# Another program order for the second layer of a two-layer hybrid decoder: score chunks, transposes and products placed by time

## The chip, the cores and the metric

The kernel runs on one core of one Trainium2 chip. Five engines work beside each other, each on its own queue of instructions: PE (TensorE: matmuls and transposes, with its weight loads shown apart as PEld), DVE (VectorE), ACT (ScalarE), POOL (GpSimd) and SP, which here issues DMAs. The metric is the device time of one execution in microseconds (us), the median over runs. A profile is of a single execution; its span is counted from its first to its last instruction.

## The reference, cut to what matters

The input is 1024 rows of 1024 numbers. Layer 1 is differential attention with eight heads. After it one K and V are projected, and layer 2 is stick-breaking attention with sixteen heads of 64, which the kernel takes in eight pairs. Both layers multiply by a SiLU gate, project and add the residual.

```python
def block(args):                      # of _stick_breaking
    i, qb = args
    qpos = i * QB + jnp.arange(QB)
    mask = kpos[None, :] < qpos[:, None]
    z = jnp.einsum('bhqd,bshd->bhqs', qb, k).astype(jnp.float32) * scale
    log_beta = jax.nn.log_sigmoid(z)
    log_1mb = jnp.where(mask, jax.nn.log_sigmoid(-z), 0.0)
    suffix = lax.cumsum(log_1mb, axis=3, reverse=True) - log_1mb
    a = jnp.where(mask, jnp.exp(log_beta + suffix), 0.0)
    return jnp.einsum('bhqs,bshe->bhqe', a.astype(v.dtype), v)
```

## The kernel before, in words

Every fp32 operand is split into a high and a low part, and a product is three matmuls (high by high, high by low, low by high). In this text a **head** of layer 2 is one pair of reference heads, c = 0 and c = 1.

**Units.** The 1024 query rows are eight blocks of 128, numbered qb. Unit m (0 to 3) takes the blocks 2m and 2m+1, and block qb has n = (qb+1)·128 columns of scores. A block over 512 columns has its scores in two chunks, later columns first (`chunks`, `scores`, L237), one chunk at a time in the one score tile of PSUM (`sc`, two banks). ACT copies a chunk into `zl` tiles (L781), POOL masks its end (L783). Then comes a chain over the whole block: DVE L790, ACT L791, ACT L792, DVE L793, the scan on DVE L795, and ACT L796, which leaves the weights a in the `zl` tile. A block up to 512 columns takes one `zl` tile for both c, a longer one takes two; there are seven (`bl`). The first instruction on a `zl` tile is a small memset on POOL (L775).

**Transposes and products.** `unit_t_b` (S below stands for a unit's scores and chain, T for this) has a step for each c and each pair t of column blocks: up to four transposes (`transposed`, L265) into one of three PSUM banks (`tr`), the high part on ACT (`th`, L271), the low part on DVE (`tl`, L272), and four matmuls into the one bank `av` (L811, L812). `th` and `tl` share three buffers. With the last pair of a c, ACT L817 and DVE L818 take the result out of `av`. A unit has 2(m+1) such pairs, a head 20. Layer 1 has the same structure with six matmuls to a pair and ten pairs a head.

**Projections.** While head h is worked on, head h+1's k, v, q and gate are projected from the layer's input (`group`, L195 to L197, 512 columns a matmul), two PSUM banks `proj`, in that order, each for both halves of the rows. A step of `group` is four of the eight parts of the inner dimension, twelve matmuls. These steps are called the fill. The tiles of k, v and q exist twice, so k of head h+1 takes the tiles that head h-1's scores read, and v the tiles that its products read. ACT (L243) and DVE (L245) take k out of PSUM.

**The order.** `run_layer` writes a program order: for each head `main` holds S and T of the units, T of a unit behind S of the next one, the last T of a head behind the first S of the next head, and `merge` mixes main and fill in proportion to costs that stand beside the steps. Layer 2's unit order is `ORDERS[2]`, (1, 3, 0, 2). `gate_mul` of head h-1 stands behind the first unit's late T in head h. This program order is not yet the order on the engines. When the program is built, a scheduler walks through it with a model of each instruction's time and gives each engine, of the instructions that are ready by that model, the one that is earliest in the program order (`hp()` moves some ahead, `later()` some back). Tiles are given out and come free in that walk too. On the chip each engine then keeps to the order it was given, and waits on semaphores.

**The end.** The last head has a list of its own (`last_order`, for layer 2 (1, 0, 3, 2)), mixed with the output projection (`OutProj`, L424 adds the residual, L436 a remainder); the output projection's own tail follows.

Of the kernel before, what the change touches and what calls it, by code (L numbers as in the profile page):

```python
# [14 lines left out]
I32 = mybir.dt.int32  # L15
AF = mybir.ActivationFunctionType
# [3 lines left out]
P = 128  # L20
# [15 lines left out]
def build(tc, ins, out):  # L36
# [9 lines left out]
         "al": 6, "bl": 7, "tb": 3, "oa": 0, "la": 0, "lb": 8, "lt": 0, "lead": 1.0, "leada": 0.02, "leadb": 0.02, "leadxa": 0.15, "leadxb": 0.1, "holda": 0, "holdb": 0, "c2": 1, "gca": 0, "gcb": 0, "prea": 2, "preb": 1, "warm": 16, "wp": 2, "hpx": -1, "nx": 1, "nk": 6, "hpo": 0, "ob": 2, "late": 400}  # L46
# [37 lines left out]
    def zat(n):  # L84
        return zt()
# [97 lines left out]
    def group(n, pairs, done):  # L183
# [3 lines left out]
        size = 4 if n > 256 else 8  # L187
# [39 lines left out]
    def scores(q, k, i, evac):  # L227

        n = (i + 1) * P
        rs_ = slice((i % 4) * P, (i % 4) * P + P)  # L230
        for off, w in reversed(chunks(n)):
# [7 lines left out]
            evac(off, w, n, pts)  # L239

# [33 lines left out]

    def v_rows(pt):
# [9 lines left out]
    def merge(main, fill, lead=0.0):  # L285
# [4 lines left out]
        while i < len(main) or j < len(fill):  # L290
# [4 lines left out]
            else:  # L295
                df += fill[j][0]
                fill[j][1]()
                j += 1

# [141 lines left out]
    def run_layer(hds, qkv, unit_s, unit_t, xT, og, op, hfs):  # L441
# [66 lines left out]
        for h in range(n - 1):  # L508
            main = []
# [12 lines left out]
        ss = unit_s(h, ma)  # L522
        main = (late + ss if B["lt"] else ss + late) + [(0.0, lambda: gate_mul(hds[h - 1], h - 1, og)),
# [72 lines left out]
    def unit_s_a(h, m):  # L596
        hd = heads_a[h]

        def s_step(qb):
            if hd.o is None:  # L600
                hd.o = [T("o", [P, HALF], B["o"]) for _ in range(2)]
                hd.at = {}
            n = (qb + 1) * P
            p = [zat(n + P), zat(n + P)]
            mn = [small(2), small(2)]

            def evac(off, w, n, pts):
                k = 0 if off == 0 else 1
                mask = mask_a[:, HALF - w:] if off + w == n else mask_a[:, 0:1].to_broadcast([P, w])
                for c in range(2):  # L610
                    dve.tensor_tensor_reduce(p[c][:, off:off + w], pts[:, c, :w], mask, 1.0, BIG, ALU.add, ALU.min,  # L611
                                             mn[c][:, k:k + 1])

            scores(hd.q[qb // 4], hd.k, qb, evac)
            s = small(2)
            for c in range(2):
                b = mn[c][:, 0:1]
                if n > 512:
                    dve.tensor_tensor(b, b, mn[c][:, 1:2], ALU.min)
                act.activation(p[c][:, :n], p[c][:, :n], AF.Exp, bias=b, scale=-1.0, accum_out=s[:, c:c + 1])  # L620
            r = small(2)
            dve.reciprocal(r, s)
            dve.tensor_tensor(r[:, 1:2], r[:, 1:2], nlam, ALU.mult)
            dve.tensor_scalar(p[0][:, :n], p[0][:, :n], r[:, 0:1], None, ALU.mult)
            dve.scalar_tensor_tensor(p[1][:, :n], p[1][:, :n], r[:, 1:2], p[0][:, :n], ALU.mult, ALU.add)
            hd.at[qb] = p[1]

        return [(4 * (qb + 1) * P * 0.42, lambda qb=qb: s_step(qb)) for qb in (2 * m, 2 * m + 1)]

    def unit_t_a(h, m):  # L630
# [3 lines left out]
        def t_step(t):  # L634
# [3 lines left out]
            for i, (kb, th, tl) in enumerate(transposed(hd.at[2 * m], hd.at[2 * m + 1], t, t == m)):  # L638
# [14 lines left out]
        return [(4 * 55 + 6 * 109 + (430 if t == m else 0), lambda t=t: t_step(t)) for t in range(m + 1)]  # L653
# [109 lines left out]
    def unit_s_b(p, m):  # L763
        hd = heads_b[p]

        def s_step(qb):
            if hd.o is None:
                hd.o = [T("o", [P, HALF], B["o"]) for _ in range(2)]
                hd.at = {}
            n = (qb + 1) * P  # L770
            heads = ((0, 1),) if n <= HALF else ((0,), (1,))
            z = [zbt() for _ in heads]
            w2 = len(heads[0]) * n
            for t in z:
                pool.memset(t[:, w2:w2 + 1], 0.0)  # L775
# [10 lines left out]
            scores(hd.q[qb // 4], hd.k, qb, evac)  # L786
            for t in z:
                zc = t[:, :w2]
                u = u4k()[:, :w2]
                dve.tensor_scalar(u.bitcast(I32), zc.bitcast(I32), -0x80000000, None, ALU.bitwise_or)  # L790
                act.activation(u, u, AF.Exp)  # L791
                act.activation(u, u, AF.Ln, bias=1.0)  # L792
                dve.scalar_tensor_tensor(u, zc, 0.0, u, ALU.min, ALU.subtract)  # L793
                ur = u[:, ::-1]
                dve.tensor_tensor_scan(ur, t[:, 1:w2 + 1][:, ::-1], ur, 0.0, ALU.add, ALU.subtract)  # L795
                act.activation(zc, u, AF.Exp, scale=-1.0)  # L796
            hd.at[qb] = [z[0][:, :n], z[0][:, n:2 * n]] if n <= HALF else [t[:, :n] for t in z]

        return [(4 * (qb + 1) * P * 0.42, lambda qb=qb: s_step(qb)) for qb in (2 * m, 2 * m + 1)]

    def unit_t_b(p, m):
# [3 lines left out]
        def t_step(c, t):  # L805
# [3 lines left out]
            for i, (kb, th, tl) in enumerate(transposed(hd.at[2 * m][c], hd.at[2 * m + 1][c], t, t == m)):  # L809
# [12 lines left out]
        return [(4 * 55 + 4 * 109, lambda c=c, t=t: t_step(c, t)) for c in range(2) for t in range(m + 1)]  # L822
# [59 lines left out]
```

## Time and profile before

| what | value |
|---|---|
| median of three runs | 1461.78 us (1460.41 to 1463.3) |
| the profiled execution | 1463.71 us |
| its span | 1461.8 us |
| mean granted TensorE clock | 0.985 of full |
| layer 1's heads, about | 60 to 690 us |
| layer 2's heads, about | 690 to 1407 us |
| output projection's tail | 1407 to 1461.8 us |

The profiled execution is 1.9 us over the median. [...] Matmuls overlap: a 512-column matmul is listed with 0.39 us, and the next one starts 0.23 us after it. So PE can be busy for the whole of a stretch and still do more or less in it; only PE's idle time, the clock and the distance of starts tell.

### The profile page before, as it was taken

The page shows a single profiled execution, that of the slowest core. Times are in us where ns is not written, and L with a number is a line of the kernel's source. Part 1 is how long each engine was busy: PE and PEld are TensorE (multiplying, and loading weights), DVE is VectorE, ACT ScalarE, POOL GpSimd, SP SyncE. Part 2 cuts the span into 40 slices and gives each one's busy share as a digit, 9 for nine tenths or more (in the row PEclk, how much of TensorE's full clock was granted, in tenths as well). Part 3 has the DMA queues.
Part 4 walks back from the last instruction along what each step waited for, and adds up shares of the span by engine and source line. Part 5 has one row for each costly group of instructions (what it writes and reads, how often), then busy time and mean ns, then how long its engine had stood idle before and what let it go on. Part 6 is the DMA issues. An engine that isn't in the chain of part 4 may idle for free.

```text
span 1461.8 us, 24434 instructions
## 1 busy us (share of the span) xinstructions
PE 1409.5 (96%) x8944; PEld 1188.5 (81%) x8944; DVE 1073.2 (73%) x2219; ACT 927.8 (63%) x1908; POOL 294.9 (20%) x545
## 2 busy tenths in 40 slices
PE   8999999999999999999999999998999999987899
PEld 7888888888888888789877777776778677776699
DVE  7576667677777776775547888878878888888952
ACT  7555556566565655442557777778777877787720
POOL 0111212121212121100011222223233232335100
PEclk9999999999999999999999999999999999998999
DMA  5111111111111115621310011110011010233512
GB/s 203 59 30 44 45 44 44 44 44 44 44 44 44 44 61 185 214 90 58 116 58 29 30 58 29 44 44 30 34 45 38 30 58 30 70 133 111 193 73 80
DMA packets 43111, 99.39 MB, mean 68 GB/s; under 512 B 4848, under 2 KB 6640, under 8 KB 41968
## 3 DMA queue, kind: packets, MB, share of 16 engines
q1 hardware_dynamic: 42992, 97.83, 19.5%
q8 instruction: 71, 1.16, 0.3%
q14 instruction: 48, 0.39, 0.1%
HBM read 74.74 MB, written 23.07 MB: 67 GB/s over the span
## 4 chain that ended last, share of the span: by engine, by line
PE 75%; DVE 12%; ACT 6%; issue 4%; DMA 2%; POOL 1%; SPq 0%; DVEq 0%; POOLq 0%; ACTq 0%
PE proj L195 18%; PE proj L196 17%; PE proj L197 17%; PE sc L237 8%; PE tr L265 5%; DVE u4k L795 4%; DVE u4k L793 2%; DVE tl L272 2%; PE av L811 2%; PE av L812 2%; PE av L642 1%; ACT u4k L791 1%; PE av L640 1%; PE av L641 1%; ACT u4k L792 1%
## 5 line engine op out<-in xcount | busy, mean ns | idle before, releaser
L195 PE MATMUL proj<-ah,w 128*128 128x512 f32 x768 | 309.0, 402 | 5.4 <-DVE kl L245 5.3
L196 PE MATMUL proj<-al,w 128*128 128x512 f32 x768 | 308.5, 402 | 0.0
L197 PE MATMUL proj<-ah,w 128*128 128x512 f32 x768 | 306.4, 399 | 0.0
L195 PE MATMUL proj<-w,ah 128*128 128x256 f32 x992 | 291.2, 294 | 5.2 <-DVE kl L424 2.7
L197 PE MATMUL proj<-w,al 128*128 128x256 f32 x992 | 285.4, 288 | 0.0
L196 PE MATMUL proj<-w,ah 128*128 128x256 f32 x992 | 285.2, 288 | 0.0
L195 PEld LDWEIGHTS proj<-w,ah 128*128 128x128 f32 x992 | 192.3, 194 | 15.6 <-DVE kl L424 4.2
L197 PEld LDWEIGHTS proj<-w,al 128*128 128x128 f32 x992 | 192.3, 194 | 1.9 <-issue 1.6
L196 PEld LDWEIGHTS proj<-w,ah 128*128 128x128 f32 x992 | 192.3, 194 | 1.9 <-issue 1.3
L195 PEld LDWEIGHTS proj<-ah,w 128*128 128x128 f32 x768 | 145.6, 190 | 41.4 <-DVE kl L245 6.6
L795 DVE TENSOR_TENSOR_SCAN u4k<-zl,u4k 128x768 f32<-128x768 f32 (+4 forms) x96 | 173.7, 1812 | 1.0
L196 PEld LDWEIGHTS proj<-al,w 128*128 128x128 f32 x768 | 145.7, 190 | 33.0 <-issue 6.4
L197 PEld LDWEIGHTS proj<-ah,w 128*128 128x128 f32 x768 | 145.7, 190 | 32.1 <-issue 4.2
L237 PE MATMUL sc<-kh,q 64*128 64x512 f32 (+2 forms) x768 | 158.2, 400 | 12.6 <-ACT zl L781 9.8
L272 DVE TENSOR_TENSOR tl<-tr,th 128x512 fp32r<-128x512 f32 (+1 forms) x240 | 145.2, 629 | 32.5 <-ACT th L271 30.6
L783 POOL TENSOR_SCALAR_AFFINE_SELECT zl<-zl 128x128 f32<-128x128 f32 (+1 forms) x96 | 81.8, 857 | 306.3 <-ACT zl L781 298.5
L271 ACT ACTIVATE th<-tr 128x512 fp32r<-128x512 f32 (+1 forms) x240 | 124.4, 553 | 28.8 <-PE tr L265 24.5
L796 ACT ACTIVATE zl<-u4k 128x768 f32<-128x768 f32 (+4 forms) x96 | 81.3, 846 | 93.8 <-DVE u4k L795 81.2
L164 ACT ACTIVATE w<-raw,cols 128x256 fp32r<-128x256 f32 x240 | 104.6, 500 | 45.8 <-PE proj L196 33.5
L265 PE MATMUL tr<-ident,zl 128*128 128x128 f32 x864 | 129.0, 277 | 3.6 <-ACT zl L796 2.0
L611 DVE CUSTOM_DVE_ANT_0 zl<-sc,mask_a 128x384 f32<-128x384 f32 (+3 forms) x192 | 99.0, 552 | 40.7 <-PE sc L237 40.5
L237 PEld LDWEIGHTS sc<-kh,q 64*128 64x128 f32 x768 | 76.0, 187 | 64.6 <-issue 17.5
(146 smaller groups left out, 2590.9 us busy)
## 6 DMA issues: line engine op xcount, KB each, us to landing
raw<-in_w_kv_dram SPq DMA_DIRECT2D x32, 256.0 KB, 2.7
raw<-in_w_b_dram SPq DMA_DIRECT2D x32, 256.0 KB, 2.7
raw<-in_w_qk_dram SPq DMA_DIRECT2D x28, 256.0 KB, 2.7
raw<-in_w_vg_dram SPq DMA_DIRECT2D x28, 256.0 KB, 2.7
og_a<-o SPq DMA_DIRECT2D x28, 256.0 KB, 2.0
og_b<-o SPq DMA_DIRECT2D x28, 256.0 KB, 2.0
raw<-in_a_w_out_dram SPq DMA_DIRECT2D x26, 256.0 KB, 2.9
raw<-in_b_w_out_dram SPq DMA_DIRECT2D x26, 256.0 KB, 2.9
```

Source lines behind the costliest of these rows:

```text
L164: act.activation(h[:, i], r, AF.Copy, scale=g)
L195: pe.matmul(box["p"], lh, rh, start=(j == 0), stop=False)
L196: pe.matmul(box["p"], lh, rl, start=False, stop=False)
L197: pe.matmul(box["p"], ll, rh, start=False, stop=last)
L237: pe.matmul(pts[:, c, :wm], q[a][HI[c], rs_], k[b][HI[c], off:off + wm], start=(a + b == 0), stop=(a == 1))
L265: pe.transpose(pt[:, o:o + P], a[:, (2 * t + b) * P:(2 * t + b + 1) * P], ident)
L271: act.activation(th[:, skip:], pt[:, skip:], AF.Copy)
L272: dve.tensor_tensor(tl[:, skip:], pt[:, skip:], f32(th[:, skip:]), ALU.subtract)
L611: dve.tensor_tensor_reduce(p[c][:, off:off + w], pts[:, c, :w], mask, 1.0, BIG, ALU.add, ALU.min, mn[c][:, k:k + 1])
L783: pool.affine_select(t3[:, :, n - P:], t3[:, :, n - P:], [[0, len(cs)], [-1, P]], ALU.is_ge, -BIG, base=-1, channel_multiplier=1)
L795: dve.tensor_tensor_scan(ur, t[:, 1:w2 + 1][:, ::-1], ur, 0.0, ALU.add, ALU.subtract)
L796: act.activation(zc, u, AF.Exp, scale=-1.0)
```

## The change

Layer 2's heads but for the last are put in order by a new function, `by_time`. It gives every step a time in units of the head's period. S steps, now one for each score chunk, begin at 0 and follow each other by their cost over the period. A unit's T begins 0.1 (`lag`) after its S has ended or when the T before it has ended, and its steps are 0.9/40 (`pace`) of a period apart. The fill is spread over the whole period by cost. Steps with a time of 1 or more go into the next head's list, less 1. `gate_mul` follows 0.02 behind the last carried T step. All is sorted by time, and that is the program order.

In both layers S is now cut by chunk (`row_steps`: the same instructions, with the first allocations in `begin` and the chain in `end`), and T by `ahead`: transposes of a pair, transposes of the next pair, then the product of the first one, and so on. Costs beside the steps change with it. A `group` step of layer 2 with more than 256 columns has two parts of the inner dimension (six matmuls). The unit order of layer 2 is now `ORDERS[10]`, (2, 3, 1, 0). In the last head's list the carried steps count 400 each. No instruction is added or taken away.

```diff
-         ... "ob": 2, "late": 400}
+         ... "ob": 10, "late": 400, "lag": 0.1, "pace": 0.9}
...
-        size = 4 if n > 256 else 8
+        size = (2 if layer[1] else 4) if n > 256 else 8
...
+    def ahead(pairs):
+
+        r = []
+        for i, (ct, tr, cv, av) in enumerate(pairs):
+            r.append((ct, tr))
+            if i:
+                r.append(pairs[i - 1][2:])
+        return r + [pairs[-1][2:]]
...
+    def by_time(unit_s, unit_t, h, order, fill, carry, gate):
+
+
+        units = [(m, unit_s(h, m)) for m in order]
+        total = sum(c for _, ss in units for c, _ in ss)
+        tf = sum(c for c, _ in fill)
+        ev = [(t - 1.0, st) for t, st in carry]
+        if gate:
+            ev.append((carry[-1][0] - 1.0 + 0.02, gate))
+        at, free = 0.0, (carry[-1][0] - 1.0 if carry else 0.0)
+        per = sum(len(unit_t(h, m)) for m in order)
+        for m, ss in units:
+            for c, st in ss:
+                ev.append((at, st))
+                at += c / total
+            t = max(at + B["lag"], free)
+            for _, st in unit_t(h, m):
+                ev.append((t, st))
+                t += B["pace"] / per
+            free = t
+        at = 0.0
+        for c, st in fill:
+            ev.append((at, st))
+            at += c / tf
+        ev.sort(key=lambda e: e[0])
+        for t, st in ev:
+            if t < 1.0:
+                st()
+        return [e for e in ev if e[0] >= 1.0]
...
         for h in range(n - 1):
+            if layer[1]:
+                late = by_time(unit_s, unit_t, h, order, fill(h + 1), late, (lambda h=h: gate_mul(hds[h - 1], h - 1, og)) if h else None)
+                steps, hold = [], 0
+                continue
...
+        if layer[1]:
+            late = [(400.0, st) for _, st in late]
...
-        return [(4 * 55 + 4 * 109, lambda c=c, t=t: t_step(c, t)) for c in range(2) for t in range(m + 1)]
+        return ahead([(4 * 109, lambda c=c, t=t: tr_step(c, t), 4 * 120, lambda c=c, t=t: av_step(c, t))
+                      for c in range(2) for t in range(m + 1)])
```

Cut out of the diff: `scores` returns its chunks as a list of (cost, step), with cost 4·w·0.42 for w columns; `unit_s_a`, `unit_s_b`, `unit_t_a` and `unit_t_b` are rewritten to these helpers with their instructions as they were.

## Rows read from the trace of the kernel before

**Rows 1.** Windows: layer 1 amid its heads, its end, layer 2's heads, the last head.
```profile
core 0: us, PE busy (x) PEld busy (x) DVE busy (x) ACT busy (x) POOL busy (x), PEclk, DMA share, GB/s
127.00:529.00 402.00, 402.00 (x2755) 346.95 (x2756) 289.65 (x823) 241.31 (x584) 79.69 (x126) 1.00 0.13 44
529.00:690.00 161.00, 154.92 (x1089) 136.83 (x1089) 112.10 (x290) 73.39 (x159) 14.04 (x25) 0.97 0.39 138
...
843.00:1323.00 480.00, 458.09 (x2572) 362.07 (x2570) 400.18 (x546) 377.33 (x686) 146.10 (x277) 0.98 0.15 49
1323.00:1407.00 84.00, 68.97 (x491) 60.84 (x491) 73.65 (x106) 57.20 (x100) 21.98 (x44) 0.94 0.40 141
```

**Rows 2.** Waits of PE from 843 to 1323: total us, times, longest us.
```profile
PE sc L237 <- ACT zl L781: 5.8, 6, 2.7
PE proj L195 <- DVE kl L245: 5.3, 4, 2.3
PE av L812 <- DVE tl L272: 4.6, 10, 1.8
PE av L811 <- ACT th L271: 2.1, 2, 1.1
```

**Rows 3.** Windows: eight us around the end of a head's period.
```profile
989.00:997.00 8.00, 4.18 (x30) 2.55 (x28) 7.84 (x11) 6.65 (x14) 3.11 (x7) 0.93 0.01 2
```

**Rows 4.** Timeline of PE, 906 to 917: start, us, what, idle before and its releaser.
```profile
907.06 0.40 PE L195 MATMUL proj<-ah,w 128*128 128x512 f32 x1
907.29 0.39 PE L196 MATMUL proj<-al,w 128*128 128x512 f32 x1
...
911.10 0.38 PE L265 MATMUL tr<-ident,zl 128*128 128x128 f32 x2
913.80 0.62 PE L195 MATMUL proj<-ah,w 128*128 128x512 f32 x1 [2.32 <-DVE kl L245]
...
915.07 0.63 PE L195 MATMUL proj<-ah,w 128*128 128x512 f32 x1
915.50 0.63 PE L196 MATMUL proj<-al,w 128*128 128x512 f32 x1
```

**Rows 5.** Windows: first and last of the four stretches at the low clock, 843 to 1323.
```profile
914.00:917.40 3.40, 3.40 (x9) 2.62 (x9) 2.19 (x5) 2.79 (x4) 0.00 (x0) 0.50 0.01 2
...
1310.00:1316.80 6.80, 6.03 (x27) 5.19 (x28) 5.59 (x8) 4.90 (x8) 3.79 (x3) 0.50 0.00 0
```

**Rows 6.** Groups by line and shape, 843 to 1323: count, busy us, mean ns, idle before.
```profile
L272 DVE TENSOR_TENSOR tl<-tr,th 128x512 fp32r<-128x512 f32 x72 | 47.2, 682 | 10.5 <-ACT th L271 9.0 <-issue 1.2
L795 DVE TENSOR_TENSOR_SCAN u4k<-zl,u4k 128x768 f32<-128x768 f32 x18 | 31.8, 1773 | 0.3
...
L793 DVE SCALAR_TENSOR_TENSOR u4k<-zl,u4k 128x768 f32<-128x768 f32 x19 | 17.8, 950 | 9.6 <-ACT u4k L792 9.6
...
L791 ACT ACTIVATE u4k<-u4k 128x768 f32<-128x768 f32 x18 | 15.0, 837 | 1.3 <-DVE u4k L790 1.2
L792 ACT ACTIVATE u4k<-u4k 128x768 f32<-128x768 f32 x18 | 14.8, 836 | 0.2
...
L796 ACT ACTIVATE zl<-u4k 128x768 f32<-128x768 f32 x17 | 14.4, 846 | 9.9 <-DVE u4k L795 9.9
...
L790 DVE TENSOR_SCALAR u4k<-zl 128x768 int32<-128x768 int32 x18 | 12.4, 694 | 1.2 <-POOL zl L783 1.0 <-ACT zl L781 0.3
```

**Rows 7.** Timeline of PE, 1204 to 1206: transposes between products and projections.
```profile
1204.70 0.38 PE L265 MATMUL tr<-ident,zl 128*128 128x128 f32 x2
1204.84 0.48 PE L195 MATMUL proj<-ah,w 128*128 128x512 f32 x1
1205.15 0.39 PE L196 MATMUL proj<-al,w 128*128 128x512 f32 x1
```

**Rows 8.** Line L775 on POOL, 843 to 1323: idle until (us, times).
```profile
  PE tr L265: 28.0, 12
```

**Rows 9.** Waits of PE in the last head, 1323 to 1407.
```profile
PE av L811 <- DVE o L818: 4.6, 3, 1.9
```

More of the change, by code (lines that the diff above doesn't have):

```diff
@@ L230, in scores, with chunk @@
         rs_ = slice((i % 4) * P, (i % 4) * P + P)
-        for off, w in reversed(chunks(n)):
+        def chunk(off, w):
             n_t[0] += 1
@@ L239, in scores, with row_steps, step @@
             evac(off, w, n, pts)
+        return [(4 * w * 0.42, lambda off=off, w=w: chunk(off, w)) for off, w in reversed(chunks(n))]
+    def row_steps(qk, qb, begin, evac, end):
+        def step(j):
+            if j == 0:
+                box["s"] = scores(*qk(), qb, evac)
+                begin()
+            box["s"][j][1]()
+            if j == len(costs) - 1:
+                end()
+        box = {}
+        costs = [4 * w * 0.42 for _, w in reversed(chunks((qb + 1) * P))]
+        return [(c, lambda j=j: step(j)) for j, c in enumerate(costs)]
     def split_rows(h, l, pt, scale):
@@ L597, in unit_s_a, with row, begin @@
         hd = heads_a[h]
[L599 to L602, printed above, removed]
+        def row(qb):
             n = (qb + 1) * P
-            p = [zat(n + P), zat(n + P)]
-            mn = [small(2), small(2)]
+            st = {}
+            def begin():
+                if hd.o is None:
+                    hd.o = [T("o", [P, HALF], B["o"]) for _ in range(2)]
+                    hd.at = {}
+                st["p"] = [zat(n + P), zat(n + P)]
+                st["mn"] = [small(2), small(2)]
             def evac(off, w, n, pts):
@@ L610, in evac, with end @@
                 for c in range(2):
[L611 to L628, printed above, removed]
+                    dve.tensor_tensor_reduce(st["p"][c][:, off:off + w], pts[:, c, :w], mask, 1.0, BIG, ALU.add, ALU.min,
+                                             st["mn"][c][:, k:k + 1])
+            def end():
+                p, mn = st["p"], st["mn"]
+                s = small(2)
+                for c in range(2):
+                    b = mn[c][:, 0:1]
+                    if n > 512:
+                        dve.tensor_tensor(b, b, mn[c][:, 1:2], ALU.min)
+                    act.activation(p[c][:, :n], p[c][:, :n], AF.Exp, bias=b, scale=-1.0, accum_out=s[:, c:c + 1])
+                r = small(2)
+                dve.reciprocal(r, s)
+                dve.tensor_tensor(r[:, 1:2], r[:, 1:2], nlam, ALU.mult)
+                dve.tensor_scalar(p[0][:, :n], p[0][:, :n], r[:, 0:1], None, ALU.mult)
+                dve.scalar_tensor_tensor(p[1][:, :n], p[1][:, :n], r[:, 1:2], p[0][:, :n], ALU.mult, ALU.add)
+                hd.at[qb] = p[1]
+            return row_steps(lambda: (hd.q[qb // 4], hd.k), qb, begin, evac, end)
+        return [st for qb in (2 * m, 2 * m + 1) for st in row(qb)]
     def unit_t_a(h, m):
@@ L764, in unit_s_b, with row, begin @@
         hd = heads_b[p]
[L766 to L769, printed above, removed]
+        def row(qb):
             n = (qb + 1) * P
             heads = ((0, 1),) if n <= HALF else ((0,), (1,))
-            z = [zbt() for _ in heads]
             w2 = len(heads[0]) * n
-            for t in z:
-                pool.memset(t[:, w2:w2 + 1], 0.0)
+            z = []
+            def begin():
+                if hd.o is None:
+                    hd.o = [T("o", [P, HALF], B["o"]) for _ in range(2)]
+                    hd.at = {}
+                for _ in heads:
+                    z.append(zbt())
+                    pool.memset(z[-1][:, w2:w2 + 1], 0.0)
             def evac(off, w, n, pt):
```

43 lines of the change are left out of this document (24 added, 19 removed).

## The prediction, made before the changed kernel was run

> **What bounds the kernel now.** I read the windows first. Amid layer 1's heads PE is busy for all of 402 us, at full clock; at that layer's end, 529 to 690, it idles 6.1 us. From 843 to 1323 in layer 2 it is busy 458.1 of 480 us, so it idles 21.9 us, and the mean clock is 0.98; in the last head it idles 15.0 of 84 us at 0.94 [rows 1]. The 768-column scan has three instructions a head (one in unit 1, two in unit 2), and 18 of them stand in that stretch [rows 6]: six heads, 80 us each. PE's work is fixed, so only its idle time, the time at the low clock and the distance of matmuls can change. DVE is busy 400 of the 480 us, 83% [rows 1]: it is next in line, not yet the bound.
>
> The waits of PE say what ends the idle time: a score matmul waits for ACT to empty the one score tile (5.8 us), a projection for k to leave PSUM (5.3), a product for its own low or high part (4.6 and 2.1) [rows 2]. The second kind comes where one head ends and the next begins: after the last transposes at 911.10 nothing starts until 913.80, and then it is a projection that waited 2.32 us for L245 [rows 4]. In another such place PE is busy 4.18 of 8 us [rows 3]. My reading: transposes, products and scores of the head were late, the fill was used up ahead of its turn, and the new k could not leave PSUM, as its tile was still read by the last scores of two heads before. That last link is read from the code; the trace shows only the wait.
>
> The low clock follows these places. [...] There are four such stretches from 843 to 1323, the last from 1310.0 to 1316.8, 20.4 us in all; PE is busy in nearly all of it [rows 5]. About 19 us of work at 0.43 in place of 0.23 costs 19·0.20/0.43, 9 us.
>
> **The change, part by part.** The sum is made against the profiled execution, 1463.7 us, and then taken 1.9 us down to the median of the three runs.
>
> *Places in the period.* A head has 4608 score columns: 1408 in unit 2, 1920 in unit 3, 896 in unit 1, 384 in unit 0. So S ends at 0.306, 0.722, 0.917 and 1. In steady state T(2) runs from 0.43 to 0.70, T(3) from 0.822 to 1.182, T(1) to 1.362, T(0) to 1.452; T steps lie 0.0225 of a period, 1.8 us, apart. Before, `merge` put T(3) right behind the small S(0), and S(2) only behind T(3).
>
> *Products behind the next transposes.* From a transpose to its product now lie two or three steps, 3.6 to 5.4 us. High and low part take at most 0.68 us each by the DVE row, L272 [rows 6], if nothing stands ahead of them. The waits of products for them, 6.7 us [rows 2], should nearly all go; I take 6. What is late next is the low part itself: `th` and `tl` share three buffers and a pair needs two, so the low part of the next pair waits on DVE until the product ahead of it has read its high part, with every later DVE instruction behind it. The next product is at least two steps off, so PE does not see it: 0, and if that cover is gone no more than the 6.7 us of today.
>
> *Scores spread, T later.* T(3) now begins 8 us after S(3) instead of as soon as it can, so T is ready at its turn, and PE need not run ahead into the fill. The waits for k and for the score tile, 11.1 us [rows 2], come from running ahead and from chunks that crowd at the one score tile. I take two thirds, 7.5 us. Bounds: nothing, if S still ends as late as the k tile is wanted (it does end at 1, with k due at 1.125), and all 11.1.
>
> *The clock.* Each low stretch follows a gap like those above. With 13.5 of 21.9 us of idle gone I take half of the 9 us: 4.5; bounds 0 and 9.
>
> *Finer steps.* T has 40 steps a head instead of 20, and the fill 32 of six matmuls instead of 16 of twelve. PE's order may break up more. At a break from transposes to a projection, the projection starts 0.03 us after the last transpose began (two from 1204.70, next start 1204.84) and the one after it 0.31 later instead of 0.23 [rows 4, 7]: what is gained goes again. I take 2 us against the change; bounds 0 and 20 more breaks for seven heads at 0.08 us, 11 us.
>
> *Seven `zl` tiles.* At a head's start the list wants eight: two for c = 1 of T(3), two each for T(1) and T(0), two for block 4. So block 4 waits until 0.115, block 5 until 0.295 instead of 0.139, block 6 until 0.385 instead of 0.306. Such waits exist already: POOL's first write of a `zl` tile waited 28.0 us for transposes, twelve times [rows 8]. PE has fill and T in the meantime: 0. One tile's chain of 768 columns is 0.69 + 0.84 + 0.84 + 0.95 + 1.77 + 0.85, 5.9 us, and a second tile adds the DVE part, 3.4 [rows 6]: 9.4 us, 0.12 of a period. Block 5 is then ready at 0.295 + 0.12 = 0.415, just ahead of T(2) at 0.43. The cover is 0.015 of a period, 1.2 us, and this is where the forecast is weakest.
>
> *The gate, the DMAs.* `gate_mul` with its four stores a head moves from behind T(2)'s carried steps to 0.45. It holds four tiles of six until then; head h's own result is first written in T(2), from 0.43: at worst a short wait of ACT. The weights' loads stay at the places of the fill, which are hardly moved. 0.
>
> *The last head.* Ten pairs are carried into it instead of six, 4 x 0.68 us more for DVE [rows 6], which is busy 73.7 of 84 us there, and four pairs of PE work for PE's 15.0 idle us [rows 1]. The largest wait there, 4.6 us for the one `av` bank to be emptied [rows 9], gets transposes of the next unit in front of it. I take a gain of 2; bounds 8 and minus 6.
>
> *Layer 1.* The cut by chunk and `ahead` are made there too, but PE has no idle time and full clock [rows 1]; fill covers any wait. 0; bounds a gain of 3 from its end, and a loss of 5.
>
> Sum: 6 + 7.5 + 4.5 - 2 + 2 = 18 us, 1463.7 - 18 = 1445.7, and on the median 1444 us.
>
> [...]
>
> **Rivals.**
>
> *Slower: the `zl` tiles decide.* Block 5 gets its tiles 0.156 late, and its chain needs more than 0.12, as DVE is shared with low parts and weights. Then T(2) slips, `zl` tiles come free later, and block 5 of the next head slips further. It decides from where T(2) is over 0.05 late: T(0) then ends past 0.5 of the next period, where the second v tile is wanted, and the fill stops too. A stretch of 0.04 of a period is 3.2 us a head, 22 us for seven heads, with none of the gains: about 1484. For it: the 28 us, the 1.2 us of cover. Against it: DVE has 80 us idle in six heads, and in the list the small units behind block 7 give the time back.
>
> *No change.* The engines' order comes from the scheduler's walk, which took ready instructions ahead before as well; the list is only a priority. Then other waits take the place of those removed, half of the 13.5 us goes, and finer breaks and the last head's DVE eat it: 1459 to 1464. For it: the k tile still comes free only at the end of S. Against it: due times 8 us behind S did not exist before.
>
> *A larger gain.* All waits go, from 843 to 1323 21.9 us idle and 9 for the clock, and 10 of the last head: 1422. Against it: DVE would be at 400 in 449 us, 89%, with chains in between.
>
> **How the numbers follow.** About 0.2%, 3 us, is what a measurement of this kernel tells from no change. My forecast, 1444 with 1432 to 1456 as its own range from the bounds, has 0.50; the larger gain 0.12; no change 0.14, of which 0.04 lies below and 0.02 above the 3 us; slower 0.24. Faster is 0.50 + 0.12 + 0.04 = 0.66, same 0.08, slower 0.24 + 0.02 = 0.26. The range runs from the larger gain's 1422 to 1478, which leaves out the far part of the slower rival.
>
> **What would show it.** Right: from the first full head of layer 2 the period falls from 80 to about 77.5 us, PE's waits on L245, L271 and L272 nearly go, low-clock stretches halve, DVE rises to 86%. Wrong: L775 waits longer for transposes than 28 us, v's L754 or L755 wait for products, gaps of over 2 us remain where heads meet, or the gain sits in layer 1 or the last head.

## The result and the profile after

The changed kernel takes 1484.42 us (1481.02 to 1485.27), the kernel before 1462.12 us beside it: 1.0149 times as long [1.013, 1.0168]. It is 22 us slower, 40 us above the forecast and 6 us above the range. The profiled execution took 1485.27 us, its span 1482.9 us.

The windows view of the changed kernel for the stretches that answer to [rows 1]: the end of layer 1's heads, six heads of layer 2, the last head. A line is a stretch of the span; (x) is the number of instructions that an engine began in it, PEclk the mean granted clock as a share of full speed.

```profile
core 0: us, PE busy (x) PEld busy (x) DVE busy (x) ACT busy (x) POOL busy (x), PEclk, DMA share, GB/s
...
529.00:705.00 176.00, 161.50 (x1143) 140.43 (x1142) 121.36 (x327) 83.40 (x182) 19.21 (x35) 0.98 0.34 122
...
857.00:1338.00 481.00, 450.71 (x2524) 360.64 (x2523) 407.56 (x544) 380.42 (x683) 143.92 (x273) 0.96 0.15 49
1338.00:1426.00 88.00, 71.06 (x507) 62.18 (x506) 75.72 (x108) 57.67 (x103) 23.10 (x48) 0.92 0.37 132
```

Six heads still take 481 us, 80.2 each, but PE idles 30.3 us in them instead of 21.9, at a lower clock. The end of layer 1 has become 15 us longer (176 us for 161), with 14.5 us idle instead of 6.1. Where the loss begins is seen best at the first k of layer 2 as ACT takes it out of PSUM. The view by source line, of the kernel before and of the changed one (op, count, duration in ns, first and last start in us):

```profile
L243 ACT ACTIVATE kh<-proj x2: 598/599/600, 713.3 to 738.5; 128x512 fp32r<-128x512 f32 x2
```

```profile
L259 ACT ACTIVATE kh<-proj x1: 599/599/599, 726.6 to 726.6; 128x512 fp32r<-128x512 f32 x1
```

At 726.6 instead of 713.3 the loss is 13.3 us, before the first score of layer 2. From there to the end of the span it is 1461.8 - 713.3 = 748.5 us before and 756.3 after.

PE's waits of the changed kernel, 857 to 1338, for [rows 2] (total us, times, longest):

```profile
PE av L890 <- DVE tl L288: 12.6, 8, 2.4
PE sc L237 <- ACT zl L854: 9.0, 6, 2.9
PE av L889 <- ACT th L287: 5.0, 4, 1.5
PE proj L197 <- DMA al<-og_b: 1.8, 1, 1.8
PE proj L195 <- DVE kl L261: 0.5, 2, 0.3
PE proj L195 <- DMA ah<-og_b: 0.5, 1, 0.5
```

The wait for k fell from 5.3 to 0.5 us. The waits of products for their low and high part, which the change was to end, rose from 6.7 to 17.6, and the score tile's from 5.8 to 9.0. New are the two waits for a DMA: `gate_mul` stores its results in `og_b`, and the output projection reads them back into `ah` and `al`. That read is issued at 1302.6, 6.8 us before the first matmul on it; in the kernel before it is issued at 1275.7, 15.4 us before, and nothing waits. In the last head the products' wait for `av` has fallen from 4.6 [rows 9] to 0.7 us, and transposes wait instead. PE's waits there, 1338 to 1426:

```profile
PE tr L281 <- DVE tl L288: 9.6, 6, 3.2
...
PE av L889 <- DVE o L896: 0.7, 1, 0.7
```

### The profile page after: what moved, and what is told of

It reads as the page before. It is cut to its first block, busy times and chain, and to the rows that moved or that the text cites. A ratio compares the mean times of both kernels' runs of the same rounds, so it can differ in the third digit from the quotient of the medians.

```text
span 1482.9 us, 24364 instructions
## 1 busy us (share of the span) xinstructions
PE 1412.1 (95%) x8944; PEld 1192.1 (80%) x8944; DVE 1082.6 (73%) x2219; ACT 930.1 (63%) x1908; POOL 295.2 (20%) x545
## 5 line engine op out<-in xcount | busy, mean ns | idle before, releaser
L287 ACT ACTIVATE th<-tr 128x512 fp32r<-128x512 f32 (+1 forms) x240 | 128.3, 551 | 40.5 <-PE tr L281 31.2
L281 PE MATMUL tr<-ident,zl 128*128 128x128 f32 x864 | 138.5, 282 | 10.5 <-DVE tl L288 9.6
L165 DVE SCALAR_TENSOR_TENSOR w<-raw,cols,w 128x256 fp32r<-128x256 f32 x240 | 118.7, 543 | 27.6 <-ACT w L164 26.7
L856 POOL TENSOR_SCALAR_AFFINE_SELECT zl<-zl 128x128 f32<-128x128 f32 (+1 forms) x96 | 85.1, 892 | 249.7 <-ACT zl L854 224.8
L685 ACT ACTIVATE zl<-zl,small 128x256 f32<-128x256 f32 (+7 forms) x128 | 98.3, 770 | 56.3 <-DVE small L684 39.6
```

The source lines that it names most:

```text
L165: dve.scalar_tensor_tensor(l[:, i], r, g, f32(h[:, i]), ALU.mult, ALU.subtract)
L281: pe.transpose(pt[:, o:o + P], a[:, (2 * t + b) * P:(2 * t + b + 1) * P], ident)
L287: act.activation(th[:, skip:], pt[:, skip:], AF.Copy)
L856: pool.affine_select(t3[:, :, n - P:], t3[:, :, n - P:], [[0, len(cs)], [-1, P]], ALU.is_ge, -BIG, base=-1, channel_multiplier=1)
```

## The experiments: layer 1

Each ratio is to the kernel before, run beside it on the same chip; its own median there was 1460.75 to 1461.27 us. The first four runs part the change by layer, and layer 1's part by its pieces.

**l1_old**: layer 1 as before, layer 2 as changed. PE's order in layer 1 is then the one of before.

```diff
-            return row_steps(lambda: (hd.q[qb // 4], hd.k), qb, begin, evac, end)
+            for _, st in scores(hd.q[qb // 4], hd.k, qb, evac):
+                st()
...
-        return ahead([(4 * 109, lambda t=t: tr_step(t), 6 * 120 + (430 if t == m else 0), lambda t=t: av_step(t)) for t in range(m + 1)])
+        return [(4 * 55 + 6 * 109 + (430 if t == m else 0), lambda t=t: t_step(t)) for t in range(m + 1)]
```

> Layer 1's steps as before (a block's scores in one step, transposes and product in one step, old costs), layer 2 as changed. Theory A: layer 1's new steps cost the 13 us by which the first k of layer 2 leaves PSUM later (713.3 to 726.6), and nothing of it is caught up: 1471 us, 1.006 of before. Rival B: layer 2's end is set by its own chains on DVE and ACT, and an earlier start is lost there: 1480 to 1485. Rival C: layer 2's new order is a gain that layer 1 hides: below 1462.

**l1_new**: the other half, layer 1 as changed and layer 2 as before (`by_time` out, order 2, steps of 4, units uncut).

```diff
-         ... "ob": 10, "late": 400, "lag": 0.1, "pace": 0.9}
+         ... "ob": 2, "late": 400}
...
-        size = (2 if layer[1] else 4) if n > 256 else 8
+        size = 4 if n > 256 else 8
...
-            if layer[1]:
-                late = by_time(unit_s, unit_t, h, order, fill(h + 1), late, (lambda h=h: gate_mul(hds[h - 1], h - 1, og)) if h else None)
```

> Layer 1's steps as changed, layer 2 as before. Theory A: layer 1 alone loses 13 us: 1475 us, 1.009 of before. Rival B: what layer 1 loses is taken up by layer 2's idle time: 1462 to 1467. Rival C: 1475 as well, so this run tells A from B alone.

**l1_costs**: the changed kernel with two figures in layer 1 put back; its cut by chunk and `ahead` stay.

```diff
-        return ahead([(4 * 109, lambda t=t: tr_step(t), 6 * 120 + (430 if t == m else 0), lambda t=t: av_step(t)) for t in range(m + 1)])
+        return ahead([(4 * 55, lambda t=t: tr_step(t), 6 * 109 + (430 if t == m else 0), lambda t=t: av_step(t)) for t in range(m + 1)])
```

> As changed, but the costs that stand beside layer 1's transposes and products are 220 and 654 again, as before, in place of 436 and 720. If the loss of layer 1 comes from the costs, which give transposes and products a larger part of the head's list: about 1472. If it comes from the split into transposes and a later product: 1484.

**l1_t_old**: layer 1's pairs as one step at the old cost, its scores still cut by chunk.

```diff
-        return ahead([(4 * 109, lambda t=t: tr_step(t), 6 * 120 + (430 if t == m else 0), lambda t=t: av_step(t)) for t in range(m + 1)])
+        return [(4 * 55 + 6 * 109 + (430 if t == m else 0), lambda t=t: t_step(t)) for t in range(m + 1)]
```

> As changed, but layer 1's transposes and product of a pair are one step again with the old cost; its scores stay cut by chunk. If the split of the pairs is what layer 1 loses by: about 1471, as with layer 1 wholly as before. If the cut of the scores by chunk loses part of it: between 1474 and 1484.

| run | us | ratio | first k of layer 2 |
|---|---|---|---|
| l1_old | 1462.04 | 1.0011 [1.0001, 1.002] | 710.2 |
| l1_new | 1483.01 | 1.0161 [1.0145, 1.0178] | 726.0 |
| l1_costs | 1464.66 | 1.0025 [1.0014, 1.0037] | 709.0 |
| l1_t_old | 1459.69 | 1.0006 [0.9992, 1.0019] | 710.8 |

The loss is in layer 1: with layer 1 as before it is gone (1484.42 - 1462.04 = 22.4 us), and with layer 2 as before it is still there. It is larger than the 13 us at the first k from which the expectations worked, so all four runs miss their numbers by 7 to 11 us, though they tell their cases apart. Nearly all of it hangs on two numbers that add no instruction: 1484.42 - 1464.66 = 19.8 us. `merge` uses them only to mix attention and fill. A pair of layer 1 counts 436 + 720 = 1156 instead of 220 + 654 = 874.

What they do to PE is seen in the windows view narrowed to one tile, 60 to 450: the second figure is PE's busy time on that tile, with the number of matmuls. The kernel before, tiles `sc`, `av`, `proj`:

```profile
60.00:450.00 390.00, 55.03 (x384) 30.47 (x384) 65.48 (x128) 0.00 (x0) 1.00 0.14 44
...
60.00:450.00 390.00, 49.01 (x300) 42.15 (x300) 9.09 (x19) 7.45 (x20) 1.00 0.14 44
...
60.00:450.00 390.00, 282.44 (x1610) 231.76 (x1609) 7.58 (x11) 23.61 (x56) 1.00 0.14 44
```

The changed kernel, the same three:

```profile
60.00:450.00 390.00, 51.93 (x366) 28.84 (x366) 62.78 (x122) 0.00 (x0) 1.00 0.13 44
...
60.00:450.00 390.00, 44.10 (x276) 38.16 (x276) 8.63 (x18) 7.15 (x19) 1.00 0.13 44
...
60.00:450.00 390.00, 289.69 (x1671) 238.46 (x1670) 7.54 (x11) 24.30 (x58) 1.00 0.13 44
```

PE is as busy as before and waits for only 0.2 us in all, so nothing shows there. But by 450 it has done 18 score matmuls and 24 products fewer, and 61 projections more: the attention is late and the fill ahead. The bill comes when the fill is used up. The windows at that place, changed kernel:

```profile
60.00:560.00 500.00, 498.88 (x3323) 424.80 (x3321) 346.91 (x978) 284.79 (x691) 91.92 (x143) 1.00 0.15 52
560.00:592.00 32.00, 22.61 (x151) 17.66 (x148) 23.91 (x68) 16.88 (x36) 6.42 (x9) 0.89 0.29 96
```

l1_costs, which is busy for all of the first stretch, in the second:

```profile
560.00:592.00 32.00, 31.18 (x249) 28.06 (x248) 27.16 (x71) 19.81 (x45) 5.06 (x9) 1.00 0.38 134
```

PE's waits of the changed kernel, 450 to 705, name what is left with nothing to cover it: DVE emptying the score tile (L675), the rotary step of q and k on POOL (L629), an addition of the output projection (L479).

```profile
PE sc L237 <- DVE small L675: 5.2, 5, 1.9
PE tr L634 <- POOL qk L629: 2.7, 1, 2.7
PE proj L195 <- DVE kl L479: 2.4, 2, 2.1
```

In these 32 us PE idles 9.4 us and the mean clock is 0.89; l1_costs idles 0.8 us at 1.00.

Three runs ask how the cost figures do it. **lead_a** is the changed kernel with the attention's list started earlier in the mix; if its lateness is the cause, that must give some of the time back. **l1_mid** and **l1_low** give a pair about half of the added cost, and less than before.

```diff
-         ... "leada": 0.02, ...}
+         ... "leada": 0.1, ...}
```

> As changed, with its costs, but layer 1's heads' list is let ahead of the fill by 0.1 of its cost instead of 0.02. Theory: with the new costs layer 1's attention falls behind the fill by some three score chunks (18 score matmuls fewer than before at 450 us), and its last head then runs with no fill left. If so, letting the list ahead by about that much gives the time back: 1463 to 1470. Rival: the new costs hurt by where single steps of the list stand to each other, not by how the list stands to the fill: 1478 to 1485.

```diff
-        return ahead([(4 * 109, ..., 6 * 120 + ...
+        return ahead([(4 * 82, ..., 6 * 114.5 + ...
```

> As changed, but the costs beside layer 1's transposes and product are 328 and 687, 1015 together, midway between 874 (1464.7 us) and 1156 (1484.4 us). If the costs act gradually: 1470 to 1479. If the loss is one outcome of the walk that is there or not: about 1464 or about 1484.

```diff
-        return ahead([(4 * 109, ..., 6 * 120 + ...
+        return ahead([(4 * 41, ..., 6 * 81 + ...
```

> As changed, but the costs beside layer 1's transposes and product are 164 and 486, 650 together, as far below the old 874 as the new 1156 lies above. If a smaller place for the scores is what hurts: 1455 to 1465, no worse than with the old costs. If any change of these costs hurts: 1470 or more.

lead_a takes 1470.13 us, 1.0064 [1.0046, 1.0082], with the first k at 718.8: some 13 of the 22 us come back by the lead alone, but only 7.8 of the 17.6 us by which the first k of the changed kernel lies behind that of l1_costs. By 450 its scores are nearly back in step (378 matmuls, 6 fewer than in the kernel before instead of 18), its products are not (276, still 24 fewer), and in 560 to 592 PE still idles 6.7 us. That speaks for the lateness as the cause, of the products as well as of the scores, and does not prove it. l1_mid takes 1462.0, 1.0002 [0.9993, 1.0011]; l1_low 1466.12, 1.0029 [1.0018, 1.004]. So the effect isn't proportional: half of the added cost costs nothing, and a cost below the old one is no better than the old one in l1_costs (1.0029 and 1.0025). By the costs themselves the list moves little. Unit 1's scores begin at 0.271 of a head's list instead of 0.251, unit 2's at 0.418 instead of 0.405, unit 3's at 0.661 instead of 0.655. With eight heads in some 630 us that is at most 1.6 us, while PE's score matmuls come later from head to head (against l1_mid by 1.4 us near 140, 11 near 237, 25 near 445). As PE waits for next to nothing up to 450 (0.2 us in all), this is the order that it was given, so the step from 1.6 to 25 us is made in the scheduler's walk. Which event of it tips the order was not found.

## The experiments: layer 2

l1_old shows that all of the change in layer 2 together is worth nothing. The next runs stand on l1_old, with one thing changed each, and ask where the expected 18 us went. Six heads of l1_old, 840 to 1320, by windows and by PE's waits:

```profile
840.00:1320.00 480.00, 451.44 (x2562) 360.49 (x2561) 410.23 (x547) 383.06 (x689) 145.42 (x276) 0.98 0.15 49
```

```profile
PE av L882 <- DVE tl L288: 13.0, 8, 2.4
PE sc L237 <- ACT zl L846: 8.9, 6, 2.9
PE av L881 <- ACT th L287: 3.7, 4, 1.4
```

It has the same waits as the changed kernel, so they belong to layer 2's new order and not to layer 1. PE idles 28.6 us here against 21.9 in the kernel before, and yet the six heads take the same 480 us: PE's busy time has fallen from 458.1 to 451.4 us for nearly the same number of matmuls (2572 and 2562), so they stand closer together. What is gained in one is lost in the other.

**noahead**: a product stands right behind its own transposes again.

```diff
-        return ahead([(4 * 109, lambda c=c, t=t: tr_step(c, t), 4 * 120, lambda c=c, t=t: av_step(c, t))
-                      for c in range(2) for t in range(m + 1)])
+        return [st for c in range(2) for t in range(m + 1) for st in
+                ((4 * 109, lambda c=c, t=t: tr_step(c, t)), (4 * 120, lambda c=c, t=t: av_step(c, t)))]
```

> Layer 1 as before, layer 2 by time, but each product right behind its own transposes, at the same spacing. If putting the product behind the next transposes takes waits for the low and high part away, these waits (16.7 us from 840 to 1320 with it) grow, and the time rises by 3 to 6 us to 1465 to 1468. If those waits come from DVE being behind as a whole and not from the distance, nothing changes: 1460 to 1464.

**size4**: steps of the fill of twelve matmuls again.

```diff
-        size = (2 if layer[1] else 4) if n > 256 else 8
+        size = 4 if n > 256 else 8
```

> Layer 1 as before, layer 2 by time, but projection steps of twelve matmuls as before. The prediction put the finer steps at 2 us against the change: 1460. If the scheduler's walk breaks steps up anyway, 1462.

**ob2**: the unit order of before, (1, 3, 0, 2).

```diff
-         ... "ob": 10, ...}
+         ... "ob": 2, ...}
```

> Layer 1 as before, layer 2 by time, but in the unit order of before, (1, 3, 0, 2), which puts a long unit at the end of the period. If the seven tiles for scores held the new order back: faster than 1462, by up to 10. If the new order's early long units are what the placing by time needs: slower, 1466 to 1475.

**merge_ahead**: from the other side, the kernel before with layer 2's transposes ahead at the old costs and with the finer steps, still mixed by cost.

```diff
-        size = 4 if n > 256 else 8
+        size = (2 if layer[1] else 4) if n > 256 else 8
...
-        return [(4 * 55 + 4 * 109, lambda c=c, t=t: t_step(c, t)) for c in range(2) for t in range(m + 1)]
+        return ahead([(4 * 55, lambda c=c, t=t: tr_step(c, t), 4 * 109, lambda c=c, t=t: av_step(c, t))
+                      for c in range(2) for t in range(m + 1)])
```

> The kernel before, with its order by cost, its unit order and its costs, and of the change only two things in layer 2: each product behind the next transposes, and projection steps of six matmuls. With the placing by time these two were worth 11 and 6 us. If they are worth that without it as well: 1445 to 1456, faster than both kernels. If they only mend what the placing by time costs: 1458 to 1466.

| run | us | ratio |
|---|---|---|
| noahead | 1473.06 | 1.0083 [1.0059, 1.0107] |
| size4 | 1468.29 | 1.0051 [1.0035, 1.0067] |
| ob2 | 1458.09 | 0.9983 [0.9973, 0.9992] |
| merge_ahead | 1465.12 | 1.0037 [1.0024, 1.0051] |

Under the new order transposes ahead are worth 11 us and the finer steps 6, more than either expectation had; under the old one both together cost 4 us (1465.12 against 1460.79 beside it). That fits the reading that what they give goes to mend what the placing by time itself costs; a run with the placing alone was not made. The new unit order costs 4 us here. Part of that may be the wait for `og_b`: every profile with the new unit order has it (0.7 to 3.5 us in all), none with the old one.

noahead does not gain its 11 us where the prediction sought them. PE's waits of noahead, 840 to 1320:

```profile
PE sc L237 <- ACT zl L846: 11.9, 7, 5.1
PE av L882 <- DVE tl L288: 10.0, 8, 2.4
PE proj L195 <- DVE kl L261: 3.6, 2, 2.9
...
PE av L881 <- ACT th L287: 1.4, 1, 1.4
```

With each product right behind its own transposes, products wait 11.4 us for their two parts, less than the 16.7 us of l1_old. What grows are the waits for the score tile and for k, and PE's idle time in all, 33.1 us for 28.6.

Two runs ask what bounds the ends of the periods. **kperm** tests the link that the prediction read from the code, that k cannot leave PSUM before the old scores are done: k has two tiles for good, its later half is projected first (q's likewise), and block 4's chunks are 512 and 128 columns.

```diff
-        return [(0, 384), (384, n - 384)] if n == 640 else [(0, 512), (512, n - 512)]
+        return [(0, 384), (384, n - 384)] if n == 640 and not layer[1] else [(0, 512), (512, n - 512)]
...
-            hd.k = (T("kh", [P, S], 2, F32R), T("kl", [P, S], 2, F32R))
+            i = heads_b.index(hd) % 2 if layer[1] else 2
+            if i == 2 or kept[i] is None:
+                hd.k = (T("kh", [P, S], 2, F32R), T("kl", [P, S], 2, F32R))
+            if i < 2:
+                kept[i] = hd.k = kept[i] or hd.k
...
-                jobs.add(lambda load=load: [load()], lambda W, fs=fs: [st for k, f in enumerate(fs) for hf in (0, 1)
+                jobs.add(lambda load=load: [load()], lambda W, fs=fs: [st for k, f in enumerate(fs) for hf in ((1, 0) if layer[1] and k == 0 else (0, 1))
```

> Layer 1 as before, layer 2 by time, but k lies in two tiles that stay for the whole layer, so that each half of a head's k waits only for the scores that read that half, and the half that units 2 and 3 alone read is projected first (q likewise); block 4's chunks are 512 and 128. Theory: what starves PE at a period's end is that both halves of the new k wait in PSUM for the last scores of two heads before. If so, v's projection fills part of the gap: 1 to 2.5 us a head, 1447 to 1456. Rival: DVE, 93% and more busy there, sets the end of the period, and PE's work only moves into the gap: 1459 to 1463.

**noabs** takes one DVE instruction a tile out of the chain, the one that sets the sign of every score. The exponential is then taken of 0 times the score, so layer 2's weights are not computed. **abs_half** moves that instruction to ACT for the second tile of long blocks.

```diff
-                    dve.tensor_scalar(u.bitcast(I32), zc.bitcast(I32), -0x80000000, None, ALU.bitwise_or)
-                    act.activation(u, u, AF.Exp)
+                    act.activation(u, zc, AF.Exp, scale=0.0)
```

> Layer 1 as before, layer 2 by time, and the first step of the chain, DVE's sign of z (0.69 us at 768 columns, 12 a head, some 8 us of DVE a head), is left out; ACT's exponential runs on z times zero in its place, so layer 2's weights are not computed. Theory: at a period's end DVE is the bound (93 to 98% busy there) and PE waits for it. Then most of the 28 us of idle from 840 to 1320 goes, with part of the low clock: 1425 to 1440. Rival: PE's gaps come from the order of tiles and buffers, and DVE is only busy beside them: 1452 to 1462.

```diff
-                    dve.tensor_scalar(u.bitcast(I32), zc.bitcast(I32), -0x80000000, None, ALU.bitwise_or)
-                    act.activation(u, u, AF.Exp)
+                    if t is z[0]:
+                        dve.tensor_scalar(u.bitcast(I32), zc.bitcast(I32), -0x80000000, None, ALU.bitwise_or)
+                    else:
+                        act.activation(u, zc, AF.Abs)
+                    act.activation(u, u, AF.Exp, scale=1.0 if t is z[0] else -1.0)
```

> Layer 1 as before, layer 2 by time; for the second tile of each long block the sign step moves from DVE to ACT (an absolute value), 4 of 12 a head, some 3 us a head. If DVE bounds the end of a period and ACT does not: 3 to 12 us faster than without it, 1450 to 1459. If ACT's queue is as tight as DVE's there (84 to 98% busy): 1460 to 1466.

kperm takes 1465.81 us, 1.0036 [1.0023, 1.0049]. PE idles 480 - 450.62 = 29.4 us in 840 to 1320, against 28.6 in l1_old. Its waits there:

```profile
PE sc L237 <- ACT zl L852: 7.5, 4, 3.2
PE proj L195 <- DVE kl L261: 4.5, 2, 2.4
```

Two waits for k of up to 2.4 us are back although an early tile was there. kperm's timeline shows why at one of them:

```profile
897.95 0.58 ACT L259 ACTIVATE kh<-proj 128x512 fp32r<-128x512 f32 x1
...
901.01 1.76 DVE L866 TENSOR_TENSOR_SCAN u4k<-zl,u4k 128x768 f32<-128x768 f32 x1
902.80 0.69 DVE L261 TENSOR_TENSOR kl<-proj,kh 128x512 fp32r<-128x512 f32 x1
...
903.55 0.50 PE L195 MATMUL proj<-ah,w 128*128 128x512 f32 x1 [2.06 <-DVE kl L261]
```

The tile was free: the high part of the first half leaves at 897.95, that of the second at 910.69, where in l1_old the two leave together (905.0 and 905.5). But the low part stands in DVE's queue behind a block's chain until 902.80. Under the new order k's tile is not the bound; the waits change their names, not their sum. The run does not lie in either range of its expectation.

noabs takes 1442.08 us, 0.987 [0.9855, 0.9884], 20 us less than l1_old and between its two cases. Its window 840 to 1320:

```profile
840.00:1320.00 480.00, 463.96 (x2686) 371.51 (x2685) 381.35 (x498) 388.24 (x709) 152.48 (x296) 0.99 0.18 60
```

With DVE at 381 us instead of 410, and a shorter chain besides, PE idles 16.0 us instead of 28.6. abs_half takes 1485.56 us, 1.0171 [1.0154, 1.0188], 23.5 us more than l1_old and 20 above the worse of its two cases. As fewer heads' work fits into 480 us of it, it is compared over the whole span, l1_old first, then abs_half, and by its waits from 840 to 1320:

```profile
0.00:1461.04 1461.04, 1404.49 (x8944) 1189.59 (x8944) 1080.97 (x2219) 930.38 (x1908) 293.70 (x545) 0.98 0.20 68
...
0.00:1482.23 1482.23, 1412.13 (x8944) 1195.19 (x8944) 1064.06 (x2187) 954.88 (x1940) 293.54 (x545) 0.98 0.20 67
```

```profile
PE av L884 <- ACT th L287: 11.0, 4, 6.2
PE sc L237 <- ACT zl L846: 8.3, 7, 4.1
```

DVE is busy 17 us less, ACT 24.5 us more, and PE now waits longest for ACT. So noabs does not show that DVE's load alone is the bound. My reading is that the queues of DVE and ACT and the chain that passes between them are one bound, and that load moved from one to the other moves the wait. DVE is busy 85% of l1_old's stretch from 840 to 1320 and ACT 80%, and moving the instruction from the one to the other did not pay. Why it costs as much as 23 us stays open; the scheduler's walk was a new one here too.

How such waits are made up is seen in the changed kernel's timeline, near 915 and near 994 (start, us, engine and line, idle before and its releaser):

```profile
914.49 1.59 POOL L218 TENSOR_TENSOR o<-g2k,o 128x512 f32<-128x512 f32 x1 [3.08 <-ACT o L217]
...
914.73 1.07 ACT L287 ACTIVATE th<-tr 128x512 fp32r<-128x512 f32 x2
914.84 2.85 DVE L868 TENSOR_TENSOR_SCAN u4k<-zl,u4k 128x768 f32<-128x768 f32 x1
...
917.72 1.89 DVE L288 TENSOR_TENSOR tl<-tr,th 128x512 fp32r<-128x512 f32 x3
...
918.46 0.39 PE L890 MATMUL av<-tl,v 128*128 128x256 f32 x1 [1.64 <-DVE tl L288]
...
992.22 0.40 PE L237 MATMUL sc<-kh,q 64*128 64x512 f32 x2
...
993.42 2.80 DVE L868 TENSOR_TENSOR_SCAN u4k<-zl,u4k 128x1024 f32<-128x1024 f32 x1
...
995.02 0.40 PE L197 MATMUL proj<-ah,w 128*128 128x512 f32 x1
...
996.26 1.06 ACT L869 ACTIVATE zl<-u4k 128x1024 f32<-128x1024 f32 x1 [1.56 <-DVE u4k L868]
...
997.22 1.01 ACT L854 ACTIVATE zl<-sc 128x1024 f32<-128x1024 f32 x1
998.28 0.39 PE L237 MATMUL sc<-kh,q 64*128 64x256 f32 x2 [2.86 <-ACT zl L854]
```

The high parts of two pairs are ready at 915.80, but DVE is in a scan of 2.85 us and comes to their low parts at 917.72; PE stands still for 1.64 us. In the second place PE has finished its last projection at 995.4. ACT could empty the score tile, whose last matmul ended at 992.62, but stands idle for 1.56 us at L869, which is ahead of L854 in its queue and waits for DVE's scan. The scan ends at 996.22, L869 and L854 follow, and PE goes on at 998.28: 2.86 us idle, of which no part is a wait for k.

## The experiments: what is left without the loss

**costs_ob2** is the changed kernel with layer 1's two costs and layer 2's unit order of before; **t_old_ob2** is l1_t_old with that unit order. The edit of the first:

```diff
-         ... "ob": 10, ...}
+         ... "ob": 2, ...}
...
-        return ahead([(4 * 109, lambda t=t: tr_step(t), 6 * 120 + (430 if t == m else 0), lambda t=t: av_step(t)) for t in range(m + 1)])
+        return ahead([(4 * 55, lambda t=t: tr_step(t), 6 * 109 + (430 if t == m else 0), lambda t=t: av_step(t)) for t in range(m + 1)])
```

> As changed, with layer 1's costs as before and layer 2's unit order as before (1, 3, 0, 2); the placing by time, the product behind the next transposes in both layers and the finer steps stay. If the two parts add: 1464.7 - 4 = 1461, no change against the kernel before.

> Layer 1's pairs as before, its scores cut by chunk, layer 2 by time in the unit order of before. If the parts add: 1459.7 - 4 = 1456, 0.997 of the kernel before, faster than both kernels.

costs_ob2 takes 1456.72 us, 0.9969 [0.9957, 0.998], and t_old_ob2 1458.1, 0.9978 [0.9966, 0.9989]. Both are faster than the kernel before, the first by 4.5 us: that is what the change is worth without the two parts that cost time. Neither is where its expectation had it (1461 and 1456), for the parts do not add: the unit order of before gives 4.0 us behind l1_old, 7.9 behind l1_costs and 1.6 behind l1_t_old. Every edit makes a new walk of the scheduler, so a difference of a few us between two of these programs need not come from the part that was edited.

## Why the prediction was wrong

The measured time lies 40 us above the forecast: 22 of them are layer 1, and 18 are the gain in layer 2, which did not come.

**Layer 1** is the step that failed first. The prediction took 0 for it, with a loss of at most 5, because PE has no idle time there and "fill covers any wait". Up to 560 the fill did cover nearly every wait (PE idles 1.1 us from 60 on). But the fill is a fixed amount of work, and what it covers early is missing at the end. The term measured 22.4 us. The two cost figures alone make 19.8 of it, 17.6 of these before the first k (726.6 against 709.0). Some of the loss comes behind the first k, and that is layer 1's too: from there to the end l1_new, with layer 2 as before, takes 1482.2 - 726.0 = 756.2 us, the kernel before 748.5. How it is carried over was not found.

**Products behind the next transposes** (gain 6): the waits of products rose by 11 us. The step is worth 11 us under the new order, but not by the mechanism that the prediction named: without it the products' waits are shorter (11.4 against 16.7 us), and those for the score tile and for k longer. The premise failed that a low part needs 0.68 us "if nothing stands ahead of them": a scan does, of 2.85 us in the timeline at 914.84. One thing in that passage, and in the account of the kernel before, was misread as well: `th` and `tl` have three buffers each, not three together. The wait of a low part for its buffer, and the loss of up to 6.7 us that hung on it, do not follow.

**Scores spread, T later** (gain 7.5): the wait for k went, 4.8 of 5.3 us. The score tile's wait grew by 3.2. The reading that k's tile holds up the projection is not borne out under the new order: in kperm that tile is free early, and k still waits for DVE. In the kernel before, the trace shows both at the place of [rows 4]:

```profile
910.19 0.40 PE L237 MATMUL sc<-kh,q 64*128 64x512 f32 x2
...
911.64 1.08 ACT L243 ACTIVATE kh<-proj 128x512 fp32r<-128x512 f32 x2
...
913.07 1.27 DVE L245 TENSOR_TENSOR kl<-proj,kh 128x512 fp32r<-128x512 f32 x2
```

The last scores end at 910.59, which the tile may have waited for; the 3.2 us from there to the projection at 913.80 pass in the queues of ACT and DVE.

**The clock** (gain 4.5) went the other way, 0.96 for 0.98. The term was half of 9 us, worked out from the starts in [rows 4]: 0.43 us apart at 915.07, 0.23 at 907.06. Idle time alone does not set the clock: from 840 to 1320 l1_old idles 28.6 us and keeps 0.98, noahead idles 33.1 at 0.97 and kperm 29.4 at 0.96.

**Finer steps** (loss 2): the wrong sign. They are worth 6 us under this order, as size4 shows. With steps of twelve matmuls fourteen products wait for their low part instead of eight (19.6 us against 13.0), but the score tile's wait is shorter (2.5 against 8.9), so what makes the 6 us is not shown.

**The gate, the DMAs** (0): the read of `og_b` behind the late `gate_mul` makes PE wait 2.3 us.

**The last head** (gain 2): the wait for `av` went, and 9.6 us for the low parts of the carried pairs came. PE idles 16.9 us instead of 15.0.

**The `zl` tiles** (0, and the slower rival): their shortage came. POOL's first write of a tile, 857 to 1338, waited for transposes twice as long as in [rows 8]:

```profile
  PE tr L281: 58.5, 21
```

But that line is in l1_costs too (53.1 us, 20 times), and it loses 3 us in all. An eighth tile, which would show their price, was not tried. The rival's 1484 is the time that was measured, by another cause. It was not right.

**No change** was the right case for layer 2: l1_old is at 1.0011, and other waits took the place of those removed. The unit order, to which no term was given, costs 4 us. The prediction looked for a bound in one tile and one wait, when the profile showed DVE busy 83% and ACT 79% of the six heads [rows 1], with queues that feed each other.

## What to carry to other kernels

Where PE is always busy, look at what it is busy with: count the matmuls of each kind up to a fixed time, since fill that ran ahead of its turn was here a loss that showed only where the fill ended (0.2 us of waits up to 450, 9.4 us idle from 560 to 592). A cost figure in a planner is part of the program (two of them made 19.8 us here): change it alone and measure it alone. When a part gives time, look whether the waits that it was made for are the ones that fell. And when one wait is removed beside queues as busy as here (DVE 83%, ACT 79%), expect that its time may come back under another name, and price a move by what the queue of the engine that takes it looks like at that place.

## What the runs showed of the hardware

A scan on DVE took longer when a tensor-by-tensor instruction on POOL had started before it and was still running. In the timeline above, L218 on POOL ends at 914.49 + 1.59 = 916.08; the scan of 768 columns, begun at 914.84, ends at 917.69, 1.6 us after that and 2.85 us after its start, where such scans took 1.77 us in the mean [rows 6]. One other scan of 768 columns in the changed kernel began so: at 1242.62, with L218 running from 1241.90 to 1243.71. It took 2.71 us and ended 1.6 us after L218; the 22 that remain took 1.74 to 1.85 us. In the other order it was POOL's instruction that took longer. A scan of 1024 columns at 1310.04 took 2.33 us, and L218, begun during it, 3.08, against 1.59 above:

```profile
1310.34 3.08 POOL L218 TENSOR_TENSOR o<-g2k,o 128x512 f32<-128x512 f32 x1
```

That the later one of the two waits for the other is my reading of these times. Such meetings explain little of the difference between the two kernels: the 72 scans of six heads take 131.7 us in the kernel before, and the changed one's 134.1 with a 73rd of 1.8 us, which belongs to the next head.
